# Sliding-window attention in a hybrid decoder step: scores of two heads in one product over block-diagonal keys, probabilities normalised in place and transposed

## The chip, the cores and the metric

One core of one Trainium2 chip runs the whole program. The metric is the device time of one execution in microseconds. The engines that matter here are TensorE (PE in the profile: matrix products; PEld is its loading of the stationary operand), VectorE (DVE), ScalarE (ACT) and GpSimd (POOL), and the DMA queue of SyncE (SP), which brings the weights.

## The reference

The program is one step of a two-layer decoder trunk over a prompt of 512 tokens and eight sequences of four new tokens. Every layer has a modulation computed from a condition vector, a combined input projection, three mixers (windowed attention, a state space part, a gated recurrence), an output projection, and a convolutional FFN. The change is in the prompt's part of the windowed attention: eight query heads in two groups of four, each group with one key and value head of 64 features, a window of 128, and a sink for each head that joins the softmax's sum:

```python
def sink_softmax_attend(q, k, v, allowed, sinks):
    s = jnp.einsum('...qkgd,...skd->...kgqs', q.astype(jnp.float32), k.astype(jnp.float32)) * (HEAD_DIM ** -0.5)
    s = jnp.where(allowed, s, -jnp.inf)
    sink = sinks.astype(jnp.float32)[..., None, None]
    m = jnp.maximum(jnp.max(s, axis=-1, keepdims=True), sink)
    p = jnp.exp(s - m)
    p = p / (jnp.sum(p, axis=-1, keepdims=True) + jnp.exp(sink - m))
    o = jnp.einsum('...kgqs,...skd->...qkgd', p, v.astype(jnp.float32))
    return o.astype(v.dtype)
```

All of it is in fp32. The queries of a block of 128 tokens see the keys of their own block and of the one before it, so the first block has 128 keys and the other three have 256.

## The kernel before

Features lie on the partitions and tokens on the columns. The wide products (L431, helper `mm3`) split both operands into a high and a low part and make three products of a cheaper type; their weights come by the SP queue into three `raw` buffers and are split there by ACT (L416) and DVE (L417). All other products are plain fp32, each of which the compiler turns into two passes of PE.

A layer's mixers run while the input projection's wide products are issued. After each of those (a "tick") the program issues, in this order, one step of the chains (q, k, v, state space, recurrence), one slab of background work, and one step of attention. The background slabs are the modulation of later parts: a 512 KB slab of `wada` in a `raw` buffer and eight products of 32 columns' width (L519). When the wide products are used up, the output projection waits (`need`, inside `proj`) and ticks go on until every mixer has delivered. A scheduler then orders each engine's instructions, so what stands next to what on PE is its decision and not only the program's.

A unit of attention is one of four pairs of query heads (`c`) and one of four blocks of tokens (`j`): 16 units a layer, 32 in all. The upper 64 partitions of `M.q[c]` hold one head, the lower 64 the other; `M.k` holds the two key heads in the same way. Attention is a pipeline of three ticks (`att_tick`):

- `att_S`: for each head a product of its 64 rows of queries and keys into a bank of its own (L1236); DVE masks it, and finds the maximum (L1239); ACT takes the exponential and its sum (L378, tile `pm`); DVE the reciprocal (L1246); ACT writes for each head an identity scaled by that reciprocal (L378, tile `dg`).
- `att_T`: each 128x128 block of probabilities as the stationary operand and its head's `dg` as the moving one (L1259): the product is the block turned and normalised in one. ACT copies it out (L1262).
- `att_V`: the turned probabilities with the values (L1274), and a copy into the place of the queries (L1276).

`pm` and `dg` have two buffers each. True transposes are used elsewhere: a product with the plain identity with PE's transpose mode set, such as L531 for the modulation and L1357 for the sample's probabilities. `k_chain` normalises and rotates the keys in place in `M.k` (the last step is L953), and stores the last 128. Neighbouring lines that the prediction speaks of are L909 (the recurrence's gates, fp32, full array) and L456 (sums of squares).

Of the kernel before, what the change touches and what calls it, by code (L numbers as in the profile page):

```python
# [58 lines left out]
DGB = 2  # L59
# [177 lines left out]
class Arena:  # L237
    """Slots of equal size, handed out and given back in program order; `kept` ones are promised to somebody."""
# [18 lines left out]
class Banks:  # L257
    """The PSUM banks, as pairs of neighbours for rows of all tokens and as single ones.

    What has been free for longest is handed out first. While `apart` is set, pairs are for the  # L260
    wide products alone and single banks for all the rest."""
# [36 lines left out]
    def one(self, w=512, wide=False, only=None):  # L298
        """Of the banks of a name that ends in `only`, where that is given and one is free."""
        for z in (only, ()):  # L300
            e = [e for e in self.free if (any(y in e[0] for y in z) if z else not self.apart or self.wide(e[0]) == wide)]
            if e:
                break
        n, b = min(e, key=lambda e: self.used[e[0]])
        self.free.remove((n, b))
        self.touch(n)
        return self.tile[n][:, b, :w]
# [10 lines left out]
def trunk(ctx: ExitStack, tc: tile.TileContext, A, O):  # L318
# [34 lines left out]
    def E(w=NT):  # L353
        return EV.get()[:, :w]
# [43 lines left out]
    class Weights:  # L398
        """The weights in the order of their use: each is split into its two parts as soon as a slot is free."""
# [33 lines left out]
    def rstd_small(ss, n, y):  # L433
        """1 / sqrt(ss / n + eps) of a few columns: a first value from the exponent's bits, then a step of third and one of second order."""
        z, t = (sp.tile([128, 40], F32, tag=f"rst{i}", name=f"rst{i}", bufs=2)[:, :ss.shape[-1]] for i in range(2))
        ts(z, ss, 1.0 / n, EPS, OP.mult, OP.add)
        ts(y.bitcast(I32), z.bitcast(I32), -0.5, 1597463007.0, OP.mult, OP.add)
        V.tensor_mul(t, y, y)
        V.tensor_mul(t, t, z)
        stt(t, t, 10.0 / 3.0, t, OP.subtract, OP.mult)  # L440
        stt(y, t, 5.0, y, OP.add, OP.mult)
        V.tensor_mul(t, y, y)
        stt(t, t, -27.0 / 1024.0, z, OP.mult, OP.mult)
        stt(y, t, 9.0 / 16.0, y, OP.add, OP.mult)

    def mean_rstd(hfs, n, squares, pin=False):
        """1 / sqrt(mean + eps) per token: a column for each block of the prompt's tokens in the halves,
        then the sample's in every row. `squares(hf)` yields a half's squares, a chunk of features at a time."""
# [19 lines left out]
    def spread(r, pin=False):  # L468
        """The prompt's part of mean_rstd in all rows of a bank, a column per token."""
# [192 lines left out]
    def emit_tab(l, h, name, ap):  # L662
        """Parks a table of the state space part in DRAM until its layer needs it."""
        scr = tc.dram_tile([128, 512], F32, name=f"tab_{name}{l}{h}")
        G.dma_start(scr, ap)
        free(ap)
        LY[l][name, h] = scr
# [9 lines left out]
    def ssm_tables(l, h):  # L677
# [21 lines left out]
        def widen(z, sign):  # L699
            """Puts the columns of either group of channels beside zeros for the other group."""  # L700
# [133 lines left out]
    def norm_stats(hf, pin=False):  # L834
        """Leaves 1 / sqrt(mean + eps) of a half's tokens, in all rows, in place of the sum of squares."""
# [36 lines left out]
    def group(products, units):  # L872
        """The first half of the tokens for some units, chunk by chunk, with the other half's norm after parts of them."""
# [60 lines left out]
    def k_chain(l, M, ps):  # L934
        pf = flat(ps)
        kw, sq, ks = M.k, E(), E()
# [16 lines left out]
        V.tensor_mul(kw[:, 0:NP], kw[:, 0:NP], nr)  # L953
        PS.put(nr)
        V.tensor_mul(kw[:, NP:NT], kw[:, NP:NT], r[:, 8:40])
        M.kready = True
        G.dma_start(O["opk"][l], kw[:, 384:512])
        G.dma_start(O["osk"][l, :, :, 124:128], seq4(kw[:, NP:NT]))
# [266 lines left out]
    def att_S(l, M, u):  # L1225
# [4 lines left out]
        ps = [one(256), one(256)]  # L1230
        pm = M.pool.tile([128, 2, 257], F32, tag="pm", name="pm", bufs=PMB)
        st = sp.tile([128, 3, 2], F32, tag="st", name="st", bufs=4)
        V.tensor_copy(pm[:, :, nk:nk + 1], d["nsink"][:, c, :, None])
        for g in range(2):
            rows = slice(64 * g, 64 * g + 64)
            T_.matmul(ps[g][:, 0:nk], M.q[c][rows, j * 128:j * 128 + 128], M.k[rows, k0:k0 + nk],  # L1236
                      start=True, stop=True)
        for g in range(2):
            V.tensor_tensor_reduce(out=pm[:, g, 0:nk], in0=ps[g][:, 0:nk], in1=M.maskp[:, 256 - nk:256],  # L1239
                                   scale=M.r[c][:, j, g:g + 1], scalar=d["nsink"][:, c, g:g + 1],  # L1240
                                   op0=OP.add, op1=OP.min, accum_out=st[:, 0, g:g + 1])
            PS.put(ps[g])
# [4 lines left out]
        dg = M.pool.tile([128, 2, 128], F32, tag="dg", name="dg", bufs=DGB)  # L1247
        for g in range(2):
            act(dg[:, g], eye, AF.Copy, scale=st[:, 2, g:g + 1])
        return pm, dg  # L1250

    def att_T(l, M, u, pm, dg):
# [3 lines left out]
        for kb in range(nb):  # L1256
            for g in range(2):
                i = kb * 2 + g
                T_.matmul(pt[:, i * 128:i * 128 + 128], pm[:, g, kb * 128:kb * 128 + 128], dg[:, g],  # L1259
                          start=True, stop=True, skip_group_check=True)  # L1260
# [25 lines left out]
    def att_tick(l, M):  # L1286
# [5 lines left out]
        if p[0] is not None:  # L1292
            u, pm = p[0]
            p[1] = (u, att_T(l, M, u, *pm))
# [19 lines left out]
    def sample_chain(l, M):  # L1314
        d = LY[l]
        k, q = M.k, M.q
# [18 lines left out]
        for B in range(2):  # L1335
            T_.matmul(ps[:, B, 128:160], qs[:, 128 * B:128 * B + 128], k[:, NP:NT], start=True, stop=True,
# [76 lines left out]
    def mixers(l, pool):  # L1413
# [11 lines left out]
        M.k = const("k", (128, NT), pool=pool)  # L1425
# [352 lines left out]
```

## Time and profile before

| | us |
|---|---|
| median of 3 runs | 1378.72 |
| lowest and highest | 1370.0 and 1390.04 |
| profiled execution, span from its first to its last instruction | 1370.1 |
| PE busy in it | 1326.9 |
| DVE busy in it | 849.6 |
| ACT busy in it | 602.4 |

The profile gives only the span of its execution, so what lies around the span is seen from the runs: the lowest of them is as long as the span itself, the median 8.6 us longer. The ends of PE's instructions are modelled and products overlap, so the busy time of a group of products adds up to more than the time that it takes; the distance from one start to the next, and the length of a piece in the chain that ended last, are better measures of what a product costs.

### The profile page before, as it was taken

Reading aid. Unit: us, or ns where it says so; the run is one execution under the profiler, and the core shown is the slowest. Engines: PE = TensorE matmul, PEld = TensorE weight load, DVE = VectorE, ACT = ScalarE, POOL = GpSimd, SP = SyncE. Lnnn points to the kernel's source line nnn. Section 1 sums busy time; section 2 is a strip of 40 time slices with the busy share of each in tenths; the row PEclk is TensorE's granted clock in tenths of the full one; section 3 lists DMA queues with packets and bytes.
Section 4 is the critical chain, followed back from the end, with each engine's and each line's share of the span. In section 5 each row is a group of like instructions: output and inputs, shape, how many; then the busy total and the mean of one; then the engine's idle time right before and its main releaser. Section 6 shows DMA issues by size and latency. Waiting matters only on the chain.

```text
span 1370.1 us, 27177 instructions
## 1 busy us (share of the span) xinstructions
PE 1326.9 (97%) x10898; PEld 1224.5 (89%) x10898; DVE 849.6 (62%) x2421; ACT 602.4 (44%) x1201; POOL 45.6 (3%) x76
## 2 busy tenths in 40 slices
PE   4899999999999999999999999999999999999998
PEld 2777876799999999999998787789999999999998
DVE  8885773678775565455576765546866456545551
ACT  4658554337552243134353555564743234313420
POOL 0111010000011000000000001000000000000000
PEclk9999998899999999999999999999999999999999
DMA  8976676343343322224235755412322322232221
GB/s 287 302 236 196 197 242 214 115 155 101 105 121 123 96 83 83 94 92 124 75 105 186 246 160 176 152 52 67 104 89 71 104 93 80 76 108 85 86 75 50
DMA packets 72399, 178.28 MB, mean 130 GB/s; under 512 B 15553, under 2 KB 26721, under 8 KB 72273
## 3 DMA queue, kind: packets, MB, share of 16 engines
q1 hardware_dynamic: 65456, 162.08, 37.6%
q0 software_dynamic: 4896, 11.68, 2.5%
q10 hardware_dynamic: 1920, 2.79, 0.7%
q8 instruction: 85, 1.39, 0.4%
q14 instruction: 42, 0.34, 0.1%
HBM read 159.37 MB, written 14.34 MB: 127 GB/s over the span
## 4 chain that ended last, share of the span: by engine, by line
PE 90%; DMA 5%; DVE 3%; ACT 1%; issue 0%; SPq 0%; ACTq 0%; DVEq 0%
PE wide L431 43%; PE fb1w L431 8%; PE fb0w L431 8%; PE fb0s L431 5%; PE fb1s L431 4%; DMA raw<-in_wada_dram 4%; PE mb1s L431 3%; PE mb0s L431 2%; PE mb0s L519 2%; PE mb1s L519 2%; PE mb0s L1259 1%; PE mb1s L1259 1%; PE mb0s L1236 1%; DVE wlo L417 1%; PE mb1s L1236 1%; PE wide L456 1%
## 5 line engine op out<-in xcount | busy, mean ns | idle before, releaser
L431 PE MATMUL wide<-hh,whi 128*128 128x256 f32 (+1 forms) x1384 | 403.9, 293 | 0.5 <-ACT sqacc L840 0.5
L431 PE MATMUL wide<-hl,whi 128*128 128x288 f32 (+1 forms) x1384 | 401.9, 290 | 0.0
L431 PE MATMUL wide<-hh,wlo 128*128 128x288 f32 (+1 forms) x1384 | 401.2, 290 | 0.0
L417 DVE TENSOR_TENSOR wlo<-raw,whi 128x1024 fp32r<-128x1024 f32 (+1 forms) x176 | 211.1, 1200 | 186.6 <-ACT whi L416 182.2
L416 ACT CAST whi<-raw 128x1024 fp32r<-128x1024 f32 (+1 forms) x176 | 180.5, 1029 | 273.4 <-PE wide L431 127.7
L431 PEld LDWEIGHTS wide<-hh,whi 128*128 128x128 f32 x1384 | 260.9, 189 | 15.0 <-issue 12.2
L431 PEld LDWEIGHTS wide<-hh,wlo 128*128 128x128 f32 x1384 | 263.0, 190 | 6.3 <-issue 5.8
L431 PEld LDWEIGHTS wide<-hl,whi 128*128 128x128 f32 x1384 | 261.0, 189 | 5.2 <-issue 4.3
L381 DVE SCALAR_TENSOR_TENSOR f<-wide,prm,f 128x511 f32<-128x511 f32 x236 | 100.2, 485 | 0.0
L431 PE MATMUL wide<-mid,whi 128*128 128x256 f32 (+1 forms) x526 | 100.0, 288 | 0.0
L431 PEld LDWEIGHTS wide<-mid,whi 128*128 128x128 f32 x526 | 82.6, 188 | 0.0
L892 ACT CAST mid<-f 128x544 fp32r<-128x544 f32 x44 | 28.5, 647 | 122.2 <-DVE f L1626 122.2
L431 PE MATMUL wide<-mid,wlo 128*128 128x256 f32 (+1 forms) x263 | 75.7, 288 | 0.0
L378 ACT ACTIVATE f<-f 128x544 f32<-128x544 f32 x50 | 33.0, 659 | 90.2 <-DVE f L1616 84.2
L431 PE MATMUL fb1w<-hh,whi 128*128 128x256 f32 (+1 forms) x240 | 69.3, 289 | 1.2 <-ACT hh L857 0.7
L431 PE MATMUL fb1w<-hl,whi 128*128 128x256 f32 (+1 forms) x240 | 69.4, 289 | 0.0
L431 PE MATMUL fb1w<-hh,wlo 128*128 128x256 f32 (+1 forms) x240 | 68.9, 287 | 0.0
L431 PE MATMUL fb0w<-hh,whi 128*128 128x256 f32 (+1 forms) x224 | 64.8, 289 | 1.2 <-ACT hh L857 0.7
L431 PE MATMUL fb0w<-hl,whi 128*128 128x256 f32 (+1 forms) x224 | 64.8, 289 | 0.0
L431 PE MATMUL fb0w<-hh,wlo 128*128 128x256 f32 (+1 forms) x224 | 64.3, 287 | 0.0
L431 PE MATMUL fb0s<-mid,whi 128*128 128x288 f32 (+1 forms) x326 | 63.1, 290 | 0.0
L431 PE MATMUL fb1s<-mid,whi 128*128 128x288 f32 (+1 forms) x308 | 59.2, 289 | 0.0
(611 smaller groups left out, 2607.9 us busy)
## 6 DMA issues: line engine op xcount, KB each, us to landing
raw<-in_wada_dram SPq DMA_DIRECT2D x92, 512.0 KB, 4.6
raw<-in_wup_dram SPq DMA_DIRECT2D x88, 512.0 KB, 3.7
raw<-in_wdn_dram SPq DMA_DIRECT2D x32, 448.0 KB, 3.3
raw<-in_win_dram SPq DMA_DIRECT2D x24, 512.0 KB, 4.3
raw<-in_wo_dram SPq DMA_DIRECT2D x16, 512.0 KB, 4.8
raw<-in_wdn_dram SPq DMA_DIRECT2D x16, 512.0 KB, 3.5
e<-q ACTq DMA_DIRECT2D x32, 68.0 KB, 4.6
out_ox_dram<-x SPq DMA_DIRECT2D x8, 272.0 KB, 2.1
```

Source lines behind the costliest of these rows:

```text
L378: return S.activation(out, in_, f, bias=bias, scale=scale, **kw)
L381: return V.scalar_tensor_tensor(out, a, s, b, op0=op0, op1=op1, **kw)
L416: S.copy(hi, raw)
L417: V.tensor_sub(lo, raw, f32(hi))
L431: T_.matmul(out, w[wi][:, k, :], r[ri][:, a:b], start=first and i == 0, stop=last and i == 2)
L456: z = T_.matmul(ps[:, 2 * i + j:2 * i + j + 1], sq[:, 128 * j:128 * j + 128], ones[:, 0:1], start=first, stop=True, skip_group_check=True)
L519: T_.matmul(ps[32 * g:32 * g + 32], silu[:, k, :], have[n][:, g], start=k == 0, stop=k == 7, skip_group_check=True)
L892: S.copy(dst[0], src)
L1236: T_.matmul(ps[g][:, 0:nk], M.q[c][rows, j * 128:j * 128 + 128], M.k[rows, k0:k0 + nk], start=True, stop=True)
L1259: T_.matmul(pt[:, i * 128:i * 128 + 128], pm[:, g, kb * 128:kb * 128 + 128], dg[:, g], start=True, stop=True, skip_group_check=True)
```

## The change

- The keys of the prompt lie in a new tile `kz` of 128 x 2 x 512: head 0's keys in the upper rows of its first plane, head 1's in the lower rows of its second, and zeros elsewhere, which POOL writes once per layer. One product of all 128 rows then gives both heads' scores beside each other in one bank. The sample's keys get a small tile `ks`. In `k_chain` the keys are worked on in a temporary tile and written to `kz` by one DVE instruction for each head; their store is split in two likewise.
- After the reciprocal DVE multiplies each head's probabilities in place; the scaled identities and their tile go.
- `att_T` uses PE's transpose with the plain identity.

```diff
     def k_chain(l, M, ps):
         pf = flat(ps)
-        kw, sq, ks = M.k, E(), E()
+        kw, sq, ks = E(), E(), E()
...
-        V.tensor_mul(kw[:, 0:NP], kw[:, 0:NP], nr)
+        for g in range(2):
+            rows = slice(64 * g, 64 * g + 64)
+            V.tensor_mul(M.kz[rows, g], kw[rows, 0:NP], nr[rows])
+            G.dma_start(O["opk"][l, rows], M.kz[rows, g, 384:512])
         PS.put(nr)
-        V.tensor_mul(kw[:, NP:NT], kw[:, NP:NT], r[:, 8:40])
-        M.kready = True
-        G.dma_start(O["opk"][l], kw[:, 384:512])
-        G.dma_start(O["osk"][l, :, :, 124:128], seq4(kw[:, NP:NT]))
+        V.tensor_mul(M.ks, kw[:, NP:NT], r[:, 8:40])
+        free(kw)
+        G.dma_start(O["osk"][l, :, :, 124:128], seq4(M.ks))
...
-        ps = [one(256), one(256)]
+        ps = one(2 * nk)
+        pv = ps.rearrange("p (g n) -> p g n", g=2)
...
+        T_.matmul(pv, M.q[c][:, j * 128:j * 128 + 128], M.kz[:, :, k0:k0 + nk], start=True, stop=True)
         for g in range(2):
-            rows = slice(64 * g, 64 * g + 64)
-            T_.matmul(ps[g][:, 0:nk], M.q[c][rows, j * 128:j * 128 + 128], M.k[rows, k0:k0 + nk],
-                      start=True, stop=True)
-        for g in range(2):
-            V.tensor_tensor_reduce(out=pm[:, g, 0:nk], in0=ps[g][:, 0:nk], in1=M.maskp[:, 256 - nk:256],
+            V.tensor_tensor_reduce(out=pm[:, g, 0:nk], in0=pv[:, g], in1=M.maskp[:, 256 - nk:256],
...
-            PS.put(ps[g])
+        PS.put(ps)
...
         V.reciprocal(st[:, 2], st[:, 1])
-        dg = M.pool.tile([128, 2, 128], F32, tag="dg", name="dg", bufs=DGB)
         for g in range(2):
-            act(dg[:, g], eye, AF.Copy, scale=st[:, 2, g:g + 1])
-        return pm, dg
-
-    def att_T(l, M, u, pm, dg):
+            ts(pm[:, g, 0:nk], pm[:, g, 0:nk], st[:, 2, g:g + 1])
+        return pm
+
+    def att_T(l, M, u, pm):
...
-                T_.matmul(pt[:, i * 128:i * 128 + 128], pm[:, g, kb * 128:kb * 128 + 128], dg[:, g],
-                          start=True, stop=True, skip_group_check=True)
+                T_.transpose(pt[:, i * 128:i * 128 + 128], pm[:, g, kb * 128:kb * 128 + 128], eye)
...
-            T_.matmul(ps[:, B, 128:160], qs[:, 128 * B:128 * B + 128], k[:, NP:NT], start=True, stop=True,
+            T_.matmul(ps[:, B, 128:160], qs[:, 128 * B:128 * B + 128], M.ks, start=True, stop=True,
...
-        M.k = const("k", (128, NT), pool=pool)
+        M.kz = const("kz", (128, 2, NP), pool=pool)
+        M.ks = const("ks", (128, NS), pool=pool)
+        for g in range(2):
+            G.memset(M.kz[64 - 64 * g:128 - 64 * g, g], 0.0)
```

On PE in layer 1, where the wide products of the input projection are used up and attention goes on tick by tick, the order before has a pair of scores, the sample's work (L1333, L1336), a transpose of the modulation, and the next unit (`raw`, `cin` and `half` are the modulation's, `vt` the values; x2 is a repeated row):

```order
L1274 MATMUL wide_70<-g_7997,vt 64x128 x4
L1259 MATMUL mb1s_7994<-dg,pm 128x128 x2
L1236 MATMUL wide_71<-k,q_8011 128x256
L1236 MATMUL mb1s_7992<-k,q_8011 128x256
L1333 MATMUL wide_70<-f_93,f_90 32x128 x4
L1333 MATMUL wide_70<-f_92,f_90 32x128 x4
L1336 MATMUL wide_70<-k,f_90 128x32 x2
L531 MATMUL mb1s_7994<-eye,half 128x128 x2
L1274 MATMUL wide_71<-f_89,vt 64x128 x2
L1236 MATMUL wide_70<-k,q_8008 128x256
L1236 MATMUL mb1s_7994<-k,q_8008 128x256
L1259 MATMUL mb1s_7992<-dg,pm 128x128 x4
```

At the same place PE has after the change (L1257 is the transpose, L1271 the product with the values, L1330 and L1333 the sample's, L530 the modulation's):

```order
L1271 MATMUL wide_70<-g_7970,vt 64x128 x4
L1257 MATMUL wide_71<-eye,pm 128x128 x2
L1236 MATMUL mb1s_7968<-kz,q_7984 128x512
L1330 MATMUL mb1s_7965<-f_93,f_90 32x128 x4
L1330 MATMUL mb1s_7965<-f_92,f_90 32x128 x4
L1333 MATMUL mb1s_7965<-ks,f_90 128x32 x2
L530 MATMUL wide_70<-eye,half 128x128 x2
L1271 MATMUL wide_71<-f_89,vt 64x128 x2
L1236 MATMUL mb1s_7965<-kz,q_7981 128x512
L1257 MATMUL mb1s_7968<-eye,pm 128x128 x4
```

Each pair of scores has become one row of twice the columns, and each product with `dg` one with `eye`; what stands between is the same.

On DVE at that place the same unit has before the change (ISA is the masked reduction, `st` the sums, `sts` and `f_90` the sample's):

```order
L1239 ISA pm,st<-wide_71,maskp,nsink,hr 128x256
L1239 ISA st 128x1
L1239 ISA pm,st<-mb1s_7992,maskp,nsink,hr 128x256
L1239 ISA st 128x1
L381 SCALAR_TENSOR_TENSOR f_90<-wide_70,masks 128x320
L538 TENSOR_TENSOR mod<-mb1s_7994,prm 128x4x18
L1246 RECIPROCAL st<-st 128x2
L1343 TENSOR_REDUCE sts<-f_90 128x2
L381 SCALAR_TENSOR_TENSOR al_9609<-mod,prm 128x18 x2
L381 SCALAR_TENSOR_TENSOR sts<-sts,nsinks 128x2
```

And after it:

```order
L1238 ISA pm,st<-mb1s_7968,maskp,nsink,hr 128x256
L1238 ISA st 128x1
L1238 ISA pm,st<-mb1s_7968,maskp,nsink,hr 128x256
L1238 ISA st 128x1
L380 SCALAR_TENSOR_TENSOR f_90<-mb1s_7965,masks 128x320
L537 TENSOR_TENSOR mod<-wide_70,prm 128x4x18
L1340 TENSOR_REDUCE sts<-f_90 128x2
L1245 RECIPROCAL st<-st 128x2
L380 SCALAR_TENSOR_TENSOR al_9569<-mod,prm 128x18
L380 SCALAR_TENSOR_TENSOR sts<-sts,nsinks 128x2
L384 TENSOR_SCALAR pm<-pm,st 128x256 x2
```

Both heads' reductions now read one bank, and the two multiplications (L384) stand behind the reciprocal, with two short rows between.

## Rows read from the trace of the kernel before

**Rows 1.** Page, part 1: span and busy time by engine.

```profile
span 1370.1 us, 27177 instructions
...
PE 1326.9 (97%) x10898; PEld 1224.5 (89%) x10898; DVE 849.6 (62%) x2421; ACT 602.4 (44%) x1201; POOL 45.6 (3%) x76
```

**Rows 2.** Page, part 4: the chain that ended last, by engine.

```profile
PE 90%; DMA 5%; DVE 3%; ACT 1%; issue 0%; SPq 0%; ACTq 0%; DVEq 0%
```

**Rows 3.** All records of the score line L1236 on PE, by bank group.

```profile
L1236 PE MATMUL mb0s<-k,q x54: 272/376/792, 86.9 to 239.8; 64*128 64x256 f32 x40, 64*128 64x128 f32 x14
L1236 PE MATMUL mb1s<-k,q x52: 272/376/480, 806.8 to 920.8; 64*128 64x256 f32 x38, 64*128 64x128 f32 x14
L1236 PE MATMUL wide<-k,q x22: 272/376/486, 216.3 to 920.8; 64*128 64x256 f32 x18, 64*128 64x128 f32 x4
```

**Rows 4.** Stretches: busy us per engine with instruction counts, clock, DMA share, GB/s.

```profile
85.00:199.00 114.00, 112.54 (x983) 88.22 (x983) 79.21 (x295) 77.14 (x179) 13.55 (x22) 1.00 0.66 205
110.00:140.00 30.00, 30.00 (x227) 22.14 (x228) 19.37 (x69) 23.60 (x51) 4.95 (x9) 1.00 0.72 218
199.00:262.00 63.00, 57.97 (x499) 39.84 (x491) 26.64 (x116) 26.22 (x83) 1.56 (x1) 0.81 0.58 189
217.00:228.00 11.00, 11.00 (x59) 7.34 (x59) 3.44 (x18) 4.90 (x17) 0.00 (x0) 0.54 0.58 181
800.00:930.00 130.00, 126.72 (x1061) 100.53 (x1061) 64.94 (x228) 77.70 (x212) 6.10 (x6) 0.96 0.40 126
```

**Rows 5.** Chain by line, shares of the stretches 84:200, 200:262, 800:930.

```profile
by line: PE wide L431 42.2%; DMA raw<-in_wada_dram 11.9%; PE mb0s L519 11.4%; PE mb0s L1259 9.3%; PE mb0s L1236 8.2%; PE mb0s L1274 5.5%; PE mb0s L909 3.8%; PE mb0s L1023 3.3%; PE mb0s L1039 2.9%; PE mb0s L1077 2.7%; PE mb0s L926 1.6%; PE m
...
by line: DMA raw<-in_wada_dram 24.5%; PE mb0s L519 19.5%; PE wide L456 6.0%; PE mb0s L1368 5.5%; PE mb0s L1259 4.8%; PE mb0s L909 4.6%; PE wide L909 3.7%; PE wide L472 3.6%; PE wide L1259 3.5%; PE wide L431 3.3%; PE wide L1236 3.1%; PE wide
...
by line: PE wide L431 23.3%; DMA raw<-in_wada_dram 15.0%; PE mb1s L1259 9.7%; PE mb1s L431 8.3%; PE mb1s L519 8.1%; PE mb1s L1236 7.3%; PE mb1s L1274 4.4%; PE mb1s L1077 3.1%; PE mb1s L909 2.8%; PE wide L1236 2.4%; PE mb1s L472 2.3%; PE wid
```

**Rows 6.** Groups of instructions: the turning's records on PE, its identities on ACT.

```profile
L1259 PE MATMUL mb1s<-dg,pm 128*128 128x128 f32 x104 | 16.5, 296 | 0.1
...
L1259 PE MATMUL mb0s<-dg,pm 128*128 128x128 f32 x100 | 15.7, 295 | 0.0
...
L378 ACT ACTIVATE dg<-eye,st 128x128 f32<-128x128 f32 x64 | 22.1, 394 | 10.4 <-DVE st L1246 10.2 <-issue 0.2
...
L1259 PE MATMUL wide<-dg,pm 128*128 128x128 f32 x20 | 4.8, 379 | 0.0
```

**Rows 7.** Chain in order of time: start us, us, what (x passes).

```profile
131.91 0.63 PE mb0s L1236 x4
...
227.97 0.22 PE wide L531 x2
...
827.40 0.22 PE mb1s L1259 x2
...
827.96 1.84 PE mb1s L909 x8
...
845.17 0.63 PE mb1s L1236 x2
```

**Rows 8.** PE in order of time up to a pair of scores: start us, us, engine, line.

```profile
131.51 0.28 PE L431 MATMUL wide<-hh,whi 128*128 128x256 f32 x1
131.63 0.28 PE L431 MATMUL wide<-hl,whi 128*128 128x256 f32 x1
131.84 0.70 PE L1236 MATMUL mb0s<-k,q 64*128 64x256 f32 x4
```

**Rows 9.** DVE: min/median/max of rows near the new operations.

```profile
L386 DVE TENSOR_SCALAR f<-f x1: 286/286/286, 4.9 to 4.9; 128x256 f32<-128x256 f32 x1
...
L953 DVE TENSOR_TENSOR k<-k,mb0s x1: 681/681/681, 77.9 to 77.9; 128x512 f32<-128x512 f32 x1
```

**Rows 10.** Chain in order of time: waits for slabs of the modulation weights.

```profile
199.32 7.46 DMA raw<-in_wada_dram
...
831.89 9.96 DMA raw<-in_wada_dram
```

More of the change, by code (lines that the diff above doesn't have):

```diff
@@ L58 @@
 PMB = 2
-DGB = 2
 SY = 2
@@ L1293, in att_tick @@
             u, pm = p[0]
-            p[1] = (u, att_T(l, M, u, *pm))
+            p[1] = (u, att_T(l, M, u, pm))
             p[0] = None
@@ L1315, in sample_chain @@
         d = LY[l]
-        k, q = M.k, M.q
+        q = M.q
         yield from slots(5)
```

## The prediction

> **What bounds the kernel now.** I read the page first: the busy shares and the chain that ended last. The span is 1370.1 us and TensorE (PE) is busy for 97% of it, VectorE (DVE) for 62%, ScalarE (ACT) for 44% [rows 1]; 90% of the chain is PE and 5% DMA [rows 2]. So an instruction taken off PE is worth its full step unless something else is late in its place. Attention runs in two places only. The score lines of layer 0 start between 86.9 and 239.8 us, those of layer 1 between 806.8 and 920.8 [rows 3]. The second view was therefore the table of stretches: in 85 to 199 PE is busy 112.5 of 114 us, in 110 to 140 without a gap, in 199 to 262 it is busy 58.0 of 63, in 800 to 930 126.7 of 130 [rows 4]. DVE is busy about two thirds of the first stretch and half of the last. Third, the chain's share by line in these stretches [rows 5]: the turning of the probabilities (L1259) has 9.3% of 116 us and 9.7% of 130 us, the scores (L1236) 8.2% and 7.3 + 2.4%. With the stretch 200 to 262 (4.8 + 3.5% of 62 us for L1259; 3.1% for L1236 in the wide banks, and by its pieces in the chain some 1.8 us in the others), and 2.0 us of L1259 in the wide banks of layer 1, L1259 carries 10.8 + 5.1 + 12.6 + 2.0 = 30.5 us of the chain and L1236 9.5 + 3.7 + 12.6 = 25.8 us. Both are nearly all on the path.
>
> **Turning the probabilities.** Before, each 128x128 block is a product with a scaled identity. There are 224 PE records of it (104 + 100 + 20) [rows 6] for 112 blocks (per head pair 2 for the first block of queries and 4 for each of the other three: 14, times 8): two passes a block. Two passes take 0.22 us in the chain at the high clock [rows 7]. The kernel already holds real transposes of 128x128: two of them (L531) take 0.22 us [rows 7]: one pass of 0.11 us a block. So 112 passes of 0.11 us go, 12.3 us. Of L1259's records 30.5 of 31 us are on the chain, so 12.2 us are worth taking off.
>
> **Scores.** Before, 128 records [rows 3] are 64 products of two passes: 48 with 256 key columns, 16 with 128. They use 64 rows of the array. A product of 256 columns alone costs 0.63 us (845.17), and a pair that stands back to back, with one head in either half of the rows, costs 0.63 us too (131.91) [rows 7]: the halves run together. Where the order parts the pair, 0.63 us is paid twice. Changing the array's shape also costs at the entry: the wide products before step by 0.12 us, the last one before a score by 0.21 [rows 8]. I count 43 entries in the timeline, 34 of them from lines that use the full array, so 34 x 0.09 = 3.1 us are paid on other lines. After, one product covers both heads, all 128 rows, 512 columns (256 for the first block). No row shows 512 columns of this type; the full-array rows nearest are the gate products, eight passes of 256 and 288 columns in 1.84 us [rows 7], 0.23 us for 272 columns, so 0.85 ns a column: 0.43 us a pass, 0.87 us for a unit of two passes, 0.43 us for the small ones. 24 x 0.87 + 8 x 0.43 = 24.3 us, against about 28.4 us of L1236's steps now (summed over the 43 places of the timeline, the first at 86.9, the last at 920.5; 25.8 on the chain), that is 22.0 us on the chain by the same share. Gain 25.8 + 3.1 - 22.0 = 6.9 us; I take off 0.6 for the six or so exits into narrower shapes that stay: 6.3 us. Ends: if every pair already ran together (24 x 0.63 + 8 x 0.42 = 18.5 us, the small ones being 0.63 less two passes of 128 columns at 0.85 ns) the merge would lose 5.8 and give back 3.1, a loss of 2.7 us; if every one stood alone (48 x 0.63 + 16 x 0.42 = 37 us) it would gain 12.7 + 3.1 = 15.8. The measured 28.4 lies between, so I stay at 6.3.
>
> In the trace a back-to-back pair costs what one costs [rows 7]. The Trainium skill's "TensorEngine Tiling (Array Packing)", section "Overview", says the same: a contraction of at most 64 rows can run as two tiles side by side, up to twice as fast. By that rule alone the merge throws a factor of two away, and the sum would be the loss of 2.7 us for the scores; the chain's 25.8 us and the entries say that the order mostly does not leave the pairs together, which is why I don't follow it.
>
> **Normalising.** ACT loses 64 scaled copies of the identity, 394 ns each, 25 us [rows 6]. DVE gains 64 multiplications in place. One row of that kind and size, 128x256, took 286 ns [rows 9]: 64 x 0.29 = 18 us at most, since 16 of them are half as wide. Neither is on the chain today (DVE 3%, ACT 1%) and DVE idles a third of the stretch, so I cost it at nothing. What hides it is that the transposes come a tick later than the scores. If that cover is gone: two copies take 0.79 us one behind the other [rows 6] and two multiplications 0.57, so the path of a unit from the sum to the transposes gets no longer. Bounds: 18 us lost if each one stood before PE; a gain is excluded, since PE idles 0.1 us and less before the records of L1259 [rows 6]. In the order of layer 1 (the rows under the change) they stand two short instructions behind the reciprocal, and PE has six rows between a unit's scores and its transposes. What queues behind these on DVE are the splits of weights, which release the raw buffers; slabs of the modulation weights mostly wait in those buffers before use. I take 0.
>
> **The rest.** Splitting the key product by head gives DVE one more instruction of 0.68 us per layer [rows 9], before the first scores, where PE has wide products: nothing, or 1.4 us at worst. POOL gets two clears per layer of 64x512 and one more DMA; no row shows such a clear, the nearest is that same 0.68 us for 128x512 on DVE. POOL is busy 3% of the span [rows 1]; behind the clears queue tables parked in DRAM in layer 0, and stores of v in layer 1, long before anybody reads them: nothing, at worst some 3 us for the four clears. One bank in place of two for the scores means DVE can begin the first head only after all 512 columns, about 0.2 us later per unit: 32 x 0.24 = 8 us if nothing covered it, nothing with PE as bound. The order keeps the attention units in the same gaps.
>
> **Sum.** 12.2 + 6.3 = 18.5 us. The span goes from 1370.1 to 1351.6 us. The runs shown lie between 1370.0 and 1390.0 with a median of 1378.7, 8.6 above this execution; I carry that over: 1360 us.
>
> **Rivals.** (1) The DMA takes part of it back. The chain holds waits for slabs of the modulation weights, 7.46 us at 199, 9.96 at 832 [rows 10] and two more of their kind in these stretches; scores and turnings that lie inside those waits are worth nothing, and a faster PE meets more of them. For it: DMA is 0.66 busy in 85 to 199. Against: in 110 to 140 PE never idles at 0.72, and each wait begins when PE has freed a buffer, so it moves with PE. Half of the gain would be left: 1370 us. (2) The clock. It is 1.00 in 85 to 199, but 0.81 over 199 to 262, with 0.54 in 217 to 228, behind waits for DMA, and 0.96 over 800 to 930 [rows 4]. At the lower of the two levels, 1.2 GHz, that is twice the missing share: 24 + 10 us. If the shorter work leaves PE emptier there and all of 199 to 262 runs at that level, its 51 us of full-speed work (39 + 24/2) take 102: 39 us more, 18.5 less, 1399 us. It is slower than before from 37 more us at the low level on. For it: four of the sixteen units of layer 0 stand there, and they get one pass instead of two. The Trainium skill's "TensorE: Matmul & The Clock Gate", section "Part 4: PE-mode transpose", says that transposes do not keep the clock up as products do; by that rule this rival gains. The existing transposes stand alone in too few places for a row to show it. (3) The other way: the units no longer change the array's shape, the waits fall elsewhere, and the 34 us at the low level go: 17 us more gained, 1343 us. (4) The merged product loses what the pairs had, as above: 12.2 - 2.7 = 9.5 us, 1369 us.
>
> **How the numbers follow.** Forecast 0.6, with a range of its own of 1350 to 1370 from the ends of the scores (4 us up, 9 down) and the runs' own scatter; rival 1 and rival 4 together 0.17; rival 2 0.06; rival 3 0.17. Two per cent of 1378.7, about what a measurement of this kernel tells from no change, is 27.6 us, so faster by that is below 1351 (rival 3 and the lower edge of the forecast): 0.2. Slower by that is above 1406, only the far part of rival 2: 0.03. Between: 0.77. The range takes in rivals 1, 3 and 4: 1342 to 1376.
>
> **What would show it.** Right: 112 records of transposes at steps of 0.11 us; 64 score records, 0.43 us each for 512 columns, with no step of 0.21 before them; no gap of PE before the transposes; the clock of 199 to 262 near 0.81. Wrong: steps of the 512-column passes well off 0.43 us; PE waiting for DVE at the transposes; longer waits for the slabs; the low clock spreading over 110 to 199 or 845 to 925.

## The result and the profile after

The changed kernel's median is 1362.7 us (7 runs, 1355.3 to 1369.4) against 1377.3 for the kernel before in the same rounds; the ratio is 0.9883, with a 95% interval of 0.9839 to 0.9926. Once more in a later call it was 0.9885 (0.9856 to 0.9913). The forecast was 1360. The profiled execution has a span of 1365.6 us.

The page after the change: the span, the engines, and the chain that ended last by engine, against [rows 1, 2].

```profile
span 1365.6 us, 26883 instructions
...
PE 1313.0 (96%) x10722; PEld 1210.7 (89%) x10722; DVE 863.1 (63%) x2487; ACT 584.0 (43%) x1138; POOL 48.9 (4%) x82
...
PE 88%; DMA 5%; DVE 4%; ACT 2%; issue 1%; POOL 0%; SPq 0%; DVEq 0%; POOLq 0%; ACTq 0%
```

The records removed are the 176 of the sum: 112 passes of the turning and 64 of the scores. TensorE is busy 13.9 us less, but the span is only 4.5 us shorter: the part of the span in which TensorE is idle rose from 43.2 to 52.6 us, and DVE and ACT have 6% of the chain against 4%. In a second profile of the changed kernel, from the later call, it is 50.5.

All records of the scores and the transposes: count, ns min/median/max, first and last start, against [rows 3, 6].

```profile
L1236 PE MATMUL mb0s<-kz,q x26: 378/592/697, 88.6 to 233.7; 128*128 128x512 f32 x20, 128*128 128x256 f32 x6
L1236 PE MATMUL mb1s<-kz,q x26: 379/592/697, 807.0 to 890.3; 128*128 128x512 f32 x18, 128*128 128x256 f32 x8
L1236 PE MATMUL wide<-kz,q x12: 437/646/1222, 214.2 to 916.8; 128*128 128x512 f32 x10, 128*128 128x256 f32 x2
...
L1257 PE MATMUL mb0s<-eye,pm x46: 270/273/476, 94.2 to 244.9; 128*128 128x128 f32 x46
L1257 PE MATMUL mb1s<-eye,pm x42: 270/273/454, 814.4 to 921.1; 128*128 128x128 f32 x42
L1257 PE MATMUL wide<-eye,pm x24: 272/289/476, 220.7 to 916.2; 128*128 128x128 f32 x24
```

64 score records and 112 transposes, as forecast. What they cost is in the chain in order of time: start us, us, line (x passes), against [rows 7].

```profile
91.77 0.86 PE mb0s L1236 x2
...
140.19 0.44 PE mb0s L1257 x4
```

A merged product of 512 columns takes 0.86 us, that is 0.43 a pass, and four transposes 0.44, that is 0.11 each: at the high clock both estimates held to a hundredth. What enters a score is in TensorE's order of time, against [rows 8]:

```profile
121.11 0.28 PE L430 MATMUL wide<-hh,wlo 128*128 128x256 f32 x1
121.23 1.02 PE L1236 MATMUL mb0s<-kz,q 128*128 128x512 f32 x2
```

The wide product before this score steps by 0.12 us. There are twelve such entries from a wide product. In six of them the wide product follows another one, and its step is 0.12 to 0.14 us; the fifteen of that kind in the kernel before took 0.21 to 0.33. In the other six it comes first after something else, and such a one takes 0.22 us in the median ahead of other wide products too.

The rest of the difference is waiting and clock. The table of stretches, with the columns of [rows 4]:

```profile
85.00:199.00 114.00, 107.75 (x958) 83.79 (x958) 87.66 (x334) 70.40 (x156) 14.18 (x23) 1.00 0.69 216
110.00:140.00 30.00, 27.20 (x207) 19.72 (x208) 21.09 (x81) 20.08 (x44) 5.02 (x9) 1.00 0.77 230
199.00:262.00 63.00, 57.63 (x475) 38.83 (x474) 33.00 (x151) 23.87 (x75) 1.56 (x1) 0.79 0.61 191
800.00:930.00 130.00, 122.74 (x997) 96.59 (x996) 73.09 (x273) 69.55 (x183) 5.82 (x6) 0.92 0.39 122
```

In 110 to 140, where TensorE had no gap before, it now idles 2.8 of 30 us. In 800 to 930 it idles 7.3 us against 3.3, and the clock is 0.92 against 0.96. All but 0.3 us of the added idle time lies in 85 to 262 and 800 to 930, where attention runs. What it waited for between 85 and 262 us: us in total, times, longest. The first and the last are of a kind that the kernel before has there too (4.7 us in four waits, and 0.5 in one); the others are new. The last four lines are of the same kind: 800 to 930 after the change, and the slabs in 85 to 262 and in 800 to 930 before it.

```profile
PE mb0s L518 <- DMA raw<-in_wada_dram: 5.7, 4, 2.8
PE mb0s L1257 <- ACT kk L730: 2.2, 1, 2.2
PE mb0s L1236 <- ACT g L750: 2.0, 1, 2.0
PE mb0s L1257 <- DVE pm L384: 0.8, 2, 0.6
PE wide L530 <- ACT half L525: 0.5, 1, 0.5
...
PE mb1s L518 <- DMA raw<-in_wada_dram: 5.0, 4, 2.2
PE mb1s L1257 <- DVE mod L537: 0.9, 1, 0.9
...
PE mb0s L519 <- DMA raw<-in_wada_dram: 4.7, 4, 1.8
PE mb1s L519 <- DMA raw<-in_wada_dram: 3.1, 3, 2.0
```

One of the gaps, 130 to 132 us, in order of time: start us, us, engine, line [idle before <- releaser].

```profile
130.38 0.16 DVE L1245 RECIPROCAL st<-st 128x2 f32<-128x2 f32 x1
130.50 1.29 DVE L1184 TENSOR_TENSOR_SCAN xc<-f,f 128x544 f32<-128x544 f32 x1
...
130.79 1.12 PE L1236 MATMUL mb0s<-kz,q 128*128 128x512 f32 x2 [1.97 <-ACT g L750]
...
131.71 0.33 DVE L384 TENSOR_SCALAR pm<-pm,st 128x256 f32<-128x256 f32 x1
...
132.03 0.34 DVE L384 TENSOR_SCALAR pm<-pm,st 128x256 f32<-128x256 f32 x1
132.09 0.14 PEld L1257 LDWEIGHTS mb0s<-eye,pm 128*128 128x128 f32 x1 [1.00 <-DVE pm L384]
```

Read it from below. The transposes wait for the multiplied probabilities; the first multiplication starts 1.2 us after the recurrence's scan (L1184, 1.29 us long), which stands between it and its reciprocal in DVE's order. And the score ahead of it had waited 1.97 us for a copy on ACT (L750). Both are chains of the other mixers. The score reads nothing that this copy writes; in the program the copy empties a bank of the group that the score is written to, so the wait is probably one for the bank.

The normalising and the transposes as groups by line: busy us, mean ns of one | idle before, and who ended it.

```profile
L377 ACT ACTIVATE pm<-pm,st 128x257 f32<-128x257 f32 (+1 forms) x64 | 30.5, 478 | 18.1 <-DVE st L1238 17.9
L384 DVE TENSOR_SCALAR pm<-pm,st 128x256 f32<-128x256 f32 (+1 forms) x64 | 19.7, 348 | 0.5
...
L384 DVE TENSOR_SCALAR pm<-pm,st 128x256 f32<-128x256 f32 x48 | 15.8, 370 | 0.4
...
L1257 PE MATMUL mb0s<-eye,pm 128*128 128x128 f32 x46 | 9.6, 300 | 3.0 <-ACT kk L730 2.2 <-DVE pm L384 0.8
L1257 PE MATMUL mb1s<-eye,pm 128*128 128x128 f32 x42 | 8.5, 299 | 0.9 <-DVE mod L537 0.9
...
L1257 PE MATMUL wide<-eye,pm 128*128 128x128 f32 x24 | 5.4, 324 | 0.5 <-DVE pm L384 0.5
```

The second line of L384 is the larger shape by itself. The exponentials cost what they did (30.6 us before); the 64 scaled identities are gone from ACT, and DVE has 19.7 us for the multiplications where 18 "at most" was forecast: the one row of that kind [rows 9] had 286 ns, the 48 of 128x256 here have 350 in the median, the 16 of 128x128 283. TensorE idles 4.4 us before the transposes, where it idled 0.1 before [rows 6]. Only 1.3 us of it (0.8 + 0.5) is waiting for the multiplication; 2.2 is for a copy of the state space chain on ACT (`kk`) and 0.9 for the modulation on DVE (`mod`). In the second profile of this kernel the three are 1.3, 2.2 and 0.9 again.

### The profile page after: what moved, and what is told of

It is laid out like the page before. It is cut to its first block, busy times and chain, and to the rows that moved or that the text cites. A ratio compares the mean times of both kernels' runs of the same rounds, so it can differ in the third digit from the quotient of the medians.

```text
span 1365.6 us, 26883 instructions
## 1 busy us (share of the span) xinstructions
PE 1313.0 (96%) x10722; PEld 1210.7 (89%) x10722; DVE 863.1 (63%) x2487; ACT 584.0 (43%) x1138; POOL 48.9 (4%) x82
## 4 chain that ended last, share of the span: by engine, by line
PE 88%; DMA 5%; DVE 4%; ACT 2%; issue 1%; POOL 0%; SPq 0%; DVEq 0%; POOLq 0%; ACTq 0%
PE wide L430 42%; PE fb1w L430 8%; PE fb0w L430 8%; PE fb0s L430 5%; PE fb1s L430 4%; DMA raw<-in_wada_dram 4%; PE mb1s L430 3%; PE mb0s L430 3%; PE mb0s L518 1%; PE mb1s L518 1%; DVE wlo L416 1%; PE mb1s L1236 1%; PE mb0s L1271 1%; PE mb1s L908 1%; PE wide L1236 1%
## 5 line engine op out<-in xcount | busy, mean ns | idle before, releaser
L430 PE MATMUL wide<-hh,whi 128*128 128x288 f32 (+1 forms) x1360 | 399.6, 295 | 0.5 <-ACT sqacc L839 0.5
L430 PE MATMUL wide<-hl,whi 128*128 128x288 f32 (+1 forms) x1360 | 397.0, 292 | 0.0
L430 PE MATMUL wide<-hh,wlo 128*128 128x288 f32 (+1 forms) x1360 | 394.8, 290 | 0.0
L430 PEld LDWEIGHTS wide<-hh,whi 128*128 128x128 f32 x1360 | 257.5, 190 | 15.0 <-issue 13.0
L430 PEld LDWEIGHTS wide<-hh,wlo 128*128 128x128 f32 x1360 | 259.0, 190 | 5.8 <-issue 5.6
L430 PEld LDWEIGHTS wide<-hl,whi 128*128 128x128 f32 x1360 | 257.7, 189 | 3.7 <-issue 3.4
```

The lines of the kernel that those rows point to most:

```text
L430: T_.matmul(out, w[wi][:, k, :], r[ri][:, a:b], start=first and i == 0, stop=last and i == 2)
```

## The experiments

Medians in us; ratios to the kernel before in the same call, with 95% intervals. The clock is the mean granted clock over all runs of a kernel; idle is the span less TensorE's busy time in the profiled execution. The kernel before had medians of 1376 to 1380 in the four calls, clock 0.980 to 0.982, idle 43.2.

| kernel | scores | turning | normalising | median | ratio | clock | idle |
|---|---|---|---|---|---|---|---|
| norm_only | by head | 2 passes | DVE | 1378.1 | 1.0011 (0.9986 to 1.0035) | 0.981 | 42.6 |
| turn_only | by head | 1 pass | DVE | 1370.6 | 0.9942 (0.9918 to 0.9966) | 0.974 | 45.2 |
| plain_turn | merged | 2 passes | DVE | 1372.6 | 0.9968 (0.9937 to 0.9998) | 0.983 | 46.5 |
| changed, again | merged | 1 pass | DVE | 1361.1 | 0.9885 (0.9856 to 0.9913) | 0.980 | 50.5 |
| pair_pin | by head, pinned | 1 pass | DVE | 1373.9 | 0.9963 (0.9933 to 0.9994) | 0.973 | 49.8 |
| act_norm | merged | 1 pass | ACT | 1367.8 | 0.9922 (0.9891 to 0.9953) | 0.980 | 52.7 |
| pool_norm | merged | 1 pass | POOL | 1380.0 | 1.0028 (0.9999 to 1.0057) | 0.977 | 61.8 |
| score_twice | merged, twice | 1 pass | DVE | 1382.2 | 1.0035 (1.0010 to 1.0059) | 0.983 | 48.2 |
| urg_soft | merged | 1 pass | DVE, ahead | 1368.7 | 0.9925 (0.9888 to 0.9962) | 0.978 | 51.4 |
| urg_all | merged, ahead | 1 pass | DVE, ahead | 1366.3 | 0.9908 (0.9876 to 0.9940) | 0.985 | 50.0 |
| norm_one | merged | 1 pass | DVE, one | 1355.1 | 0.9832 (0.9789 to 0.9875) | 0.985 | 49.7 |
| norm_one, again | merged | 1 pass | DVE, one | 1353.3 | 0.9804 (0.9766 to 0.9841) | 0.986 | 48.2 |

### The change taken apart: three kernels

`turn_only` keeps the keys, the two score products and their banks of the kernel before, and takes only the multiplication in place and the transposes. `plain_turn` is the whole change with a product in place of the transpose:

```diff
-                T_.transpose(pt[:, i * 128:i * 128 + 128], pm[:, g, kb * 128:kb * 128 + 128], eye)
+                T_.matmul(pt[:, i * 128:i * 128 + 128], pm[:, g, kb * 128:kb * 128 + 128], eye,
+                          start=True, stop=True, skip_group_check=True)
```

`norm_only` is `turn_only` with that same edit, so that of the kernel before only the normalising is changed.

> The change's turning and normalising alone: scores as before, two products over 64 rows. Theory (passes of PE are worth their step): 112 passes of 0.11 us fewer, 12 us faster than before (ratio 0.991), the turning's records 112 at steps of 0.11 us, the score records still 128 with some 28 us of steps. Rival (transposes let the clock fall): no faster than before, and the mean granted clock lower by 0.01 or more than in the kernel with plain products.

> The whole change, but the blocks are turned by plain products with the identity in place of transpose mode: two passes a block again. Theory: 224 records of turning, 12 us slower than the changed kernel and 6 us faster than before (ratio 0.995). Rival (transposes let the clock fall): as fast as the changed kernel or faster, with a mean granted clock over the runs higher by 0.01 than its 0.980.

> Keys, scores and the order of the kernel before; VectorE multiplies the probabilities in place, and the blocks are turned by plain products with the identity (two passes each, as before). With it the four combinations of two edits are there: separate or merged scores, two passes or one for turning. Theory (the passes that go are the gain, the normalising is free): ScalarE's busy time falls by 25 us and VectorE's rises by 16, TensorE has 224 turning records as before, and the time stays within 3 us of the kernel before, 1375 to 1381. Rival (the normalising stands before the turning, in VectorE's queue behind other work): TensorE waits for the multiplied probabilities, 4 to 10 us slower, 1382 to 1388. Second rival (the shorter path on ScalarE is part of the gain): 1370 to 1374. The clock: if the transposes are what lowered the mean granted clock of the kernel with the turning alone (0.974 against 0.980), it is back at 0.980 here; if it is where the normalising stands, it is near 0.974 here too.

Each against its expectation: `turn_only` gains 8 us and not 12, and its clock is 0.006 lower and not 0.01; `plain_turn` is where its theory put it; `norm_only` stays at the time and clock of the kernel before, and neither of its rivals came.

The four corners give each part twice, by differences of ratios (0.9883 for the changed kernel) times 1378 us, each 5 to 7 us either way. Normalising in DVE alone: 0.0011, +1.5 us (-1.9 to +4.8), nothing that can be told. Turning in one pass: 0.0069, 9.5 us, where the scores are by head, 0.0085, 11.7 us, where they are merged. Merging: 0.0043, 5.9 us, with two passes of turning, 0.0059, 8.1 us, with one. The two ways differ by 2.2 us, so no cross term can be told from the scatter.

### Two score products side by side

`turn_only`, and TensorE may not move one head's product away from the other's:

```diff
-            T_.matmul(ps[g][:, 0:nk], M.q[c][rows, j * 128:j * 128 + 128], M.k[rows, k0:k0 + nk],
-                      start=True, stop=True)
+            tc.keep_in_program_order(T_.matmul(ps[g][:, 0:nk], M.q[c][rows, j * 128:j * 128 + 128],
+                                               M.k[rows, k0:k0 + nk], start=True, stop=True))
```

> Turning and normalising of the change, scores as before, but the two score products of a unit pinned in program order, so that 30 of 32 pairs stand back to back. Theory (a back-to-back pair costs what one costs): score steps 24 x 0.63 + 8 x 0.42 = 18.5 us and 3 us of entries, 3 us less than the changed kernel's 24.3 at the high clock: 15 to 21 us faster than before (ratio 0.985 to 0.989), equal to or a little faster than the changed kernel. Rival (the merge is what matters): 6 us slower than the changed kernel, as turning alone.

Two pieces of its chain, a pair together and two of a pair parted (start us, us, line x passes):

```profile
116.93 0.63 PE mb0s L1236 x4
...
123.59 0.63 PE mb0s L1236 x2
124.81 0.63 PE mb0s L1236 x2
```

30 of the 32 pairs stand together in its trace, 17 in `turn_only`, and the steps of the scores, from each start to the next, add up to 26.3 us against 29.8; without the idle time that lies in these steps (3.6 and 0.3) it is 22.6 against 29.4. So the two halves of the array do run together, and the passes saved are there. The Trainium skill's "TensorEngine Tiling (Array Packing)", section "Overview", has products with a dimension of at most 64 as up to twice as fast in tiles. The trace agrees: 0.63 us for a pair and for one product of a parted pair. The time is not there: 1373.9 against 1370.6, no faster, with 49.8 us of idle against 45.2. By passes alone, 6.8 us, the pinned pairs should have caught up with the merge, as the theory had it; they did not. The added idle time took back 4.6 us. Whether it comes from the pairs or from the pin, which may hold more of the order than these two products, was not tried.

### What a merged product costs in its place

```diff
         T_.matmul(pv, M.q[c][:, j * 128:j * 128 + 128], M.kz[:, :, k0:k0 + nk], start=True, stop=True)
+        T_.matmul(pv, M.q[c][:, j * 128:j * 128 + 128], M.kz[:, :, k0:k0 + nk], start=True, stop=True)
```

> The whole change, with each merged score product issued twice into the same bank, so that the second overwrites the first: 32 products, 64 passes more, 24 x 0.86 + 8 x 0.43 = 24.1 us of TensorE's work at the high clock. It prices the merged product by itself, at the place where it stands. Theory (TensorE is the bound at the scores, so a microsecond of passes is a microsecond of time): 20 to 26 us above the changed kernel, 1382 to 1389. Rival (the units of attention lie partly beside waits of TensorE for slabs, tables and the exponentials): 8 to 16 us above, 1370 to 1378; then taking passes off the scores gives back about half of their length too, and that would be why the merge gave 2 us and not 6. The clock: the added work may fill stretches of low clock; compare at equal granted clock.

0.0150 above the changed kernel in the same call, 20.7 us (5 either way) for 24.1 us of passes, at a clock of 0.983 against 0.980; at one clock, by an estimate of 10 us for each 0.01 (below), it is some 24 us. So TensorE is the bound at this place, and the rival (8 to 16 us) falls. Its idle time is 48.2 us, little below the 50.5 of the changed kernel, so the added passes did not fill the gaps.

### Who normalises

`act_norm` and `pool_norm` differ from the changed kernel in one line:

```diff
-            ts(pm[:, g, 0:nk], pm[:, g, 0:nk], st[:, 2, g:g + 1])
+            act(pm[:, g, 0:nk], pm[:, g, 0:nk], AF.Copy, scale=st[:, 2, g:g + 1])
```
```diff
+            G.tensor_scalar(pm[:, g, 0:nk], pm[:, g, 0:nk], st[:, 2, g:g + 1], None, OP.mult)
```

> The whole change, but ACT and not DVE multiplies the probabilities in place. Theory (the engine that normalises is off the path): within 3 us of the changed kernel (ratio to before 0.986 to 0.991). Rival (DVE's 64 multiplications of some 0.35 us are paid where PE waits at the transposes): 5 us or more faster than the changed kernel (ratio below 0.985).

> The whole change, but GpSimd multiplies the probabilities in place and not VectorE. GpSimd is busy for 3% of the span. Theory (in the changed kernel TensorE idles some 9 us more than before, and part of it, about 5 us by the rows, is the turning waiting for ScalarE's and VectorE's queues): with a free engine the waits for VectorE at the transposes go, TensorE idles 2 to 4 us less, and the time is 0 to 4 us below the changed kernel's, 1358 to 1363. Rival (GpSimd is slower at it than VectorE, and its queue holds DMA issues that wait for their data): a multiplication takes over 0.5 us against 0.27, TensorE waits for GpSimd at the transposes, and the time is 3 to 15 us above the changed kernel's.

POOL's group, and one row of TensorE's waits between 85 and 262 us in that kernel:

```profile
L1247 POOL TENSOR_SCALAR pm<-pm,st 128x256 f32<-128x256 f32 (+1 forms) x64 | 63.2, 996 | 139.6 <-DVE st L1245 75.4 <-DVE hr L380 20.9 <-DVE rst L438 8.8
```
```profile
PE mb0s L1257 <- POOL pm L1247: 7.1, 11, 1.4
```

A multiplication takes 996 ns there in the mean and not 348; TensorE waits for it at eleven transposes of layer 0, 7.1 us, and in all groups and both layers 14.5 us in 23 waits. The kernel is as slow as the one before, 18.9 us above the changed kernel: the rival, and more than its 3 to 15 us. The 64 instructions are 0.65 us longer each, 41 us in all, and nearly half of that became time: the step has some cover, and a thin one. With ACT it is about 5 us worse than with DVE (ratios 0.9922 and 0.9884, intervals that overlap): a little outside its theory, and the rival, that DVE's part is paid for, falls.

### The order of the softmax

`urg_soft` puts the part of `att_S` behind the product under `with urgent():` (a higher priority for the scheduler), `urg_all` the whole of `att_tick`. `norm_one` has one multiplication for both heads:

```diff
-        for g in range(2):
-            ts(pm[:, g, 0:nk], pm[:, g, 0:nk], st[:, 2, g:g + 1])
+        V.tensor_mul(pm[:, :, 0:nk], pm[:, :, 0:nk], st[:, 2, :, None].to_broadcast([128, 2, nk]))
```

> The whole change, with the softmax of a unit (the masked reductions, the exponentials, the reciprocal and the multiplications) issued at a higher priority, so that the scheduler puts it ahead of the state space and recurrence chains in VectorE's and ScalarE's queues. TensorE idles some 6 to 9 us more in the changed kernel than in the kernel before. Theory (those waits come from the softmax queueing behind the chains): TensorE idles 3 to 6 us less, no wait at the transposes for VectorE's multiplied probabilities, 1355 to 1359, that is a ratio to the kernel before of 0.983 to 0.986 against the changed kernel's 0.988. Rival (what is taken from the waits at the transposes comes back as waits for the chains that now stand behind): idle time as before, ratio 0.987 to 0.991.

> The whole change, with all of a unit's attention (products and transposes on TensorE too) at the higher priority. Theory of the queue: the same gain as with the softmax alone, ratio 0.983 to 0.987. Rival: TensorE's own instructions move ahead too and then wait for their operands at the head of its queue, so it idles more than in the changed kernel: ratio 0.990 to 0.997.

> The whole change, with one multiplication for both heads of a unit (512 columns, the reciprocals spread over the columns) in place of two of 256 on VectorE: 32 instructions for 64. Theory (VectorE's work for the normalising is not on the path): within 3 us of the changed kernel, ratio 0.986 to 0.991, whatever one costs. Rival (it is on the path): 0.68 us for 128x512 by the rows of before against 2 x 0.27, so 0.14 us later for each of 24 units: up to 4 us slower, ratio 0.990 to 0.992.

> The kernel with one multiplication for both heads once more. It was 24.7 us below the kernel before in its call (ratio 0.9832, interval 0.9789 to 0.9875), with a mean granted clock of 0.9845 against 0.980 of the changed kernel. If the better time belongs to the order of its instructions: ratio 0.980 to 0.987 and a clock of 0.983 to 0.986 again. If it was the chance of six runs: ratio 0.987 to 0.990 and a clock near 0.980, as the changed kernel had in two calls (0.9883 and 0.9885).

Priority did not pay: in `urg_soft` TensorE still waits for DVE's multiplications (2.2 us in three waits between 85 and 262 us), its idle time is 51.4 us, and the time is 0.9925. The waits for `kk` and for L750 are gone, and those for slabs are 12.9 us in both layers against 10.7. That is the rival's case (the waits move), a little above its range. `urg_all` is at 0.9908, within the rival's range but with no more idle time than the changed kernel, so not for the rival's reason.

`norm_one` is faster than both kernels, in two calls, and neither its theory nor its rival had that. Against the changed kernel it is 0.0066 by the means of the two ratios each, 9 us. Its multiplication, by shape: busy us and mean ns of one.

```profile
L1246 DVE TENSOR_TENSOR pm<-pm,st 128x512 f32<-128x512 f32 x24 | 16.5, 689 | 0.3
L1246 DVE TENSOR_TENSOR pm<-pm,st 128x256 f32<-128x256 f32 x8 | 3.4, 424 | 0.1
```

DVE works as long for it (19.9 us) as for the 64 (19.7), so it is not DVE's time that was saved. What differs is the order around it, some 2 us less idle time, and a clock of 0.985 and, in the second call, 0.986 against 0.980. Which row of the order does it was not tried.

## Why the prediction was right

**The total.** 18.5 us were forecast, the ratios give 0.0116 x 1378 = 16 us. 1360 against 1362.7. The range's three rivals stayed small. The range itself has a slip: it gives the scores' worse end as 4 us up, where the text's own numbers, a gain of 6.3 and a loss of 2.7, make it 9; the rest of it stands in rival 4.

**Turning, 12.2 us.** Measured 9.5 and 11.7 us, by the two ways through the corners: right within the intervals. The passes, 0.11 us each, are as forecast; at one granted clock it is a little more (below).

**Scores, 6.3 us.** Measured 5.9 and 8.1 us: right within the intervals, and the two prices in the working came as given: 0.43 us a pass, and no step of 0.21 us between a run of wide products and a score. How much of the gain is these passes and how much is clock is another matter (below). Rival 4 (the merge throws away what pairs had) fell: at either way of turning the merge gains, and where the pairs are kept together by hand the kernel is 11 us slower than the merged one (0.9963 less 0.9885, times 1378) instead of faster. It did not fall by the price of the product: without idle time the scores' steps are 22.6 us with the pinned pairs and 25.6 in the changed kernel. The pinned kernel has a clock of 0.973 against 0.980; against the kernel before in the same call it is 0.0059 lower than the merged one, by an estimate of 10 us for each 0.01 (below) some 6 of the 11 us. The other 5 stay open. In its premise it was half right: 18 of the 32 pairs of the kernel before stood together.

**Normalising, 0.** Measured +1.5 us, not distinguishable from 0, where scores and turning are as before. ACT's busy time falls by 18.4 us and not by 25: the count times the mean of [rows 6] counts twice where instructions overlap, and that row's own busy time is 22.1. In the whole change the term is nearly right: TensorE waits 1.3 us for the multiplication, a sign that the prediction had named against itself. In the wait shown a short instruction is queued behind a long one, the scan of 1.29 us at 130.5. The other new waits in attention, 3.1 us before the transposes and 2.0 before a score, are for ACT's and DVE's work on other chains; the sum put such waits at nothing ("the order keeps the attention units in the same gaps"). All of them together are of the size of what the sum is off by (18.5 less 16), or more; that they are its cause is argued, not shown: with the softmax first, in `urg_soft`, those for `kk`, `mod` and L750 went, the idle time stayed, and the time was no better.

**The rest, 0.** TensorE waits for the slabs 5.7 us in 85 to 262 against 4.7, and in 800 to 930 5.0 against 3.1, which would be 3 us for rival 1. But the second profile of the same kernel has 5.5 and 2.2, no more than before: rival 1 is not shown.

**The base.** The span was forecast at 1351.6 and is 1365.6, while the median is 2.7 us off. The 8.6 us by which the median of before stood above its profile were carried over as if they were a constant. Only 1.8 us of them are one (a run's time less the span of its core, in nearly every run). For the rest they were the clock: that execution had a mean granted clock of 0.988, the runs of before 0.980. The execution profiled after has 0.975, its kernel's runs 0.980. Over 29 runs of the kernel before in one call the time falls by 9.5 us for each 0.01 of clock, over the 13 of the changed kernel by 10.9 (8.1 to 12.6 for the kernel before in the other calls). So the two profiles are some 13 us apart by clock alone, and the difference of their spans, 4.5 us, is less than a third of the change. By the mean clocks the changed kernel's profile has some 68 us at the low level and the one before some 33; of the 35 us more, two stretches of 10 us each, 23.8 to 34.0 and 40.8 to 51.1, lie ahead of the first score, so more than half of it is not attention's. Where the low stretches lie changes from one execution to the next: in the second profile 199 to 262 has 0.86 and not 0.79.

**The clock as a term.** Rivals 2 and 3 did not come: the mean of the changed kernel is 0.980 in both calls, against 0.980 to 0.982 before. Inside that stand two terms of opposite sign. Taken against the kernel before in the same call, the mean clock is 0.0012 lower in `norm_only`, 0.0063 in `turn_only` and 0.0017 in the changed kernel, and 0.0022 higher in `plain_turn`. So turning in one pass lowers it by 0.0051 with the scores by head and by 0.0039 with merged scores (standard errors 0.002). The Trainium skill's "TensorE: Matmul & The Clock Gate", section "Part 4: PE-mode transpose", says that transposes do not hold the clock up; both pairs point that way. That it is the transposes, and not that TensorE has less to do, is not shown. And merging raises the clock by 0.0034 and 0.0046.

At one clock, with 10 us for each 0.01, the turning would be worth 9.5 + 5.1 = 14.6 us and 11.7 + 3.9 = 15.6, the merge 5.9 - 3.4 = 2.5 and 8.1 - 4.6 = 3.5. One straight line through all the runs of the experiments, with a constant for each kernel and each call, gives the same: 15 and 14 for the turning, 3 and 2 for the merge, about 3 us either way. This is an estimate and leans on a fit and not on a kernel of its own. If it holds, the sum of 18.5 is right at one clock, but its two terms are some 3 us off in opposite directions, and that they make up for each other is luck. For the merge the idle time may be why: it is 4 to 5 us more with merged scores than by head (46.5 against 42.6 us, 50.5 against 45.2). That is argued, not shown.

## What to carry to other kernels

When a kernel is bound by one engine, price a removed instruction by its step in the chain; here the total came true to 2.5 us. Then look whether the queues that fed the engine can follow, since here 13.9 us less of busy time came with 9.4 us more of idle time. Before comparing two spans on a TensorE-bound kernel, compare their granted clocks: 0.01 was worth 10 us of 1370. And try the same edit in two or three spellings: kernels that differ only in how the multiplication is written, whether DVE or ACT does it, and how early softmax or attention is put in the order lay between 0.980 and 0.993.

## What was not expected of the hardware

The scatter of the runs goes with the clock: the correlation of time and mean granted clock over the 13 runs of the changed kernel is -0.88. A multiplication in place of 128x256 on DVE took 326 ns at the least and 350 in the median (128x128: 274 and 283), but one in each of the two profiles of the changed kernel took 1.37 and 1.35 us, for no reason that the profile shows. The same on POOL took 1088 ns in the mean for 128x256, against 370 on DVE. A product in two halves of the array saved its passes when it was kept together (22.6 against 29.4 us of steps without idle time) and brought no time.
